# A fused LoRA matmul in five chunks of rows in place of six, with the weights loaded ahead of the first rows

## The chip, the cores and the metric

The kernel runs on one core of a Trainium2 chip. The metric is device time in microseconds (us), the median of several executions. One more execution is recorded by the hardware profiler; its span runs from the first to the last instruction, and its time on the device is a little longer than the span.

## The reference

`x` has 16 × 2048 = 32,768 rows of 256 fp32 numbers, `W` is 256 × 256, `lora_A` 256 × 16, `lora_B` 16 × 256, `lora_E` has 16 numbers, and `scale` is 1.0.

```python
x_flat = x.reshape(-1, in_dim)
y = x_flat @ W
lora_out = x_flat @ lora_A
lora_out = lora_out * lora_E
lora_out = lora_out @ lora_B
y = y + scale * lora_out
```

The output has the shape and type of `x`. So 33.55 MB are read, 33.55 MB are written, and the matmuls between them are small.

## The kernel before

**The mathematics.** The low-rank part is folded into the weights once: `weff = W + A diag(E·scale) B`, in bf16 (lines 148 to 167). After that the kernel is one matmul, `x @ weff`.

**Rows and chunks.** `PLAN` (line 5) cuts the 256 row groups into chunks. A row group is one row for each of the 128 partitions, 1 KB a partition, 131,072 bytes in all. A chunk of `b` row groups takes `b × 128` successive rows of `x`; partition p gets `b` neighbouring rows, so that a chunk is one run of `b` KB in each partition (line 51). In this text "48 rows" means 48 row groups, as in the plan. `PIECES` (line 7) cuts the load of a chunk into several DMAs: chunk 0 comes as 16 and 32 rows, chunk 2 as 24 and 24.

**Slots.** `SLOTS` (line 9) are the buffers in SBUF. A chunk is loaded into a slot, and its result is written over it there, so a slot is free again when its store has landed. `LEAD = 4` is the number of slots: chunks 0 to 3 are loaded at the start, chunk 4 goes into the slot of chunk 0, chunk 5 into that of chunk 1.

**The order of the DMAs** is written out by hand. All loads of x and all stores are issued by SP, and run in its queue one behind another. At the start come the first piece of chunk 0 (line 114), W (115), the second piece of chunk 0 (119) and chunks 1 to 3 (120, 121). The three small tensors go through ScalarE's queue (116 to 118). Later SP waits for each chunk's last result and issues its store (223, 224); `AFTER = {1: [4, 5]}` (line 11) says that right behind store 1 it waits until store 0 has landed, issues load 4, waits until store 1 has landed, and issues load 5 (225 to 227).

**Steps.** Compute goes in 32 steps of `S = 8` rows. In each step t:

- VectorE rounds 8 rows to bf16, `rounded(t)`, line 141. Where a loaded piece begins there, it waits for that piece's load (135).
- TensorE transposes them, seen as 32-bit words, into PSUM, `transposed`, line 180.
- VectorE copies the transposed words to SBUF, `copied(t)`, line 145.
- TensorE multiplies them by `weff`, 16 matmuls, `multiplied`, line 191.
- ScalarE copies the result out of PSUM into the slot, in two halves, line 214.

VectorE takes its work in the order written: round 0, the weights' sum, round 1, and then copy t, round t+2 for each t (164 to 172). TensorE transposes step t+1 ahead of multiplying step t (201 to 204), and the first multiplication waits for the sum of the weights (199).

**HOLD** (line 13, used at 136 to 140) makes VectorE stop ahead of rounding step 14 until store 1 has landed.

**The weights.** VectorE rounds `lora_B` (149), TensorE transposes `lora_A` (153), VectorE scales it by E (`ate`, 157), TensorE multiplies the two (162), and VectorE adds W (`weff`, 167), after a wait for W's load.

Of the kernel before, what the change touches and what calls it, by code (L numbers as in the profile page):

```python
# [3 lines left out]

PLAN = [48, 32, 48, 32, 48, 48]

PIECES = {0: [16, 32], 2: [24, 24]}

SLOTS = [48, 48, 48, 32]
LEAD = 4  # L10
AFTER = {1: [4, 5]}

HOLD = 14, 1

# [19 lines left out]
def kernel(tc, x, W, lora_A, lora_B, lora_E, scale, out):  # L34
# [6 lines left out]
    KC = K // P  # L41
    assert K == M and sum(PLAN) * P == N
    starts = [sum(PLAN[:i]) * P for i in range(len(PLAN))]

    steps = [(i, r) for i, b in enumerate(PLAN) for r in range(0, b, S)]
    NS = len(steps)
    assert NS % 2 == 0

    def rows_of(flat, i):
        b, r0 = PLAN[i], starts[i]  # L50
        return flat[r0:r0 + b * P, :].rearrange("(p b) k -> p b k", b=b)

    def sbuf(name, shape, dt):
        return nc.alloc_sbuf_tensor(name, shape, dt).ap()
# [3 lines left out]

    slots = [sbuf(f"xy{s}", [P, rows, K], FP32) for s, rows in enumerate(SLOTS)]
    a_sb = sbuf("a_sb", [P, KC, R], FP32)  # L60
# [21 lines left out]
    pieces = {}  # L82
    for i, b in enumerate(PLAN):
        parts = PIECES.get(i, [b])
        pieces[i] = [(sum(parts[:j]), n) for j, n in enumerate(parts)]
    s_ld = {(i, r): Count(nc, f"s_ld{i}_{r}") for i in pieces for r, n in pieces[i]}
    s_st = [Count(nc, f"s_st{i}") for i in range(len(PLAN))]
    s_id, s_set, s_v, s_t, s_m, s_y = (
# [7 lines left out]
    def slot(i):  # L96
        return slots[i % LEAD][:, :PLAN[i], :]

    def load(i, parts=None):
        for r, n in parts or pieces[i]:  # L100
            s_ld[i, r].by(nc.sync.dma_start(out=slot(i)[:, r:r + n, :], in_=rows_of(x_flat, i)[:, r:r + n, :]), 16)  # L101

    def store(i):
        s_st[i].by(nc.sync.dma_start(out=rows_of(out_flat, i), in_=slot(i)), 16)
# [6 lines left out]


    with tc.tile_critical(no_gpsimd_drain=True):  # L113
        load(0, pieces[0][:1])
        s_w.by(nc.sync.dma_start(out=w_sb, in_=W.rearrange("(p c) m -> p c m", c=KC)), 16)  # L115
        s_a.by(nc.scalar.dma_start(out=a_sb, in_=lora_A.rearrange("(p c) r -> p c r", c=KC)), 16)
        s_b.by(nc.scalar.dma_start(out=b_sb, in_=lora_B), 16)
        s_e.by(nc.scalar.dma_start(out=e_sb, in_=lora_E[:, None]), 16)
        load(0, pieces[0][1:])
        for i in range(1, LEAD):  # L120
            load(i)
    tc.close()
# [9 lines left out]
    def rounded(t):  # L132
        i, r = steps[t]
        if (i, r) in s_ld:
            nc.vector.wait_ge(s_ld[i, r].sem, 16)
        if t == HOLD[0]:

            for _ in range(10):
                nc.vector.engine_nop()
            nc.vector.wait_ge(s_st[HOLD[1]].sem, 16)  # L140
        nc.vector.tensor_copy(out=xb[t % 2], in_=slot(i)[:, r:r + S, :]).then_inc(can_t[t % 2], 1)  # L141
# [19 lines left out]
    for c in range(KC):  # L161
        aeb_done = nc.tensor.matmul(ps_aeb[:, c, :], ate[:, c, :], b_bf, start=True, stop=True)  # L162
    s_set.by(aeb_done)
    rounded(0)
    nc.vector.wait_ge(s_w.sem, 16)
    nc.vector.wait_ge(s_set.sem, 2)
    s_v.by(nc.vector.tensor_add(out=weff, in0=w_sb, in1=ps_aeb))  # L167
    rounded(1)
    for t in range(NS):
        copied(t)  # L170
# [39 lines left out]
    for i, r in [(i, r + g) for i, r in steps for g in range(0, S, G)]:  # L210
# [7 lines left out]
        else:  # L218
# [5 lines left out]
            store(i)  # L224
            for later in AFTER.get(i, []):
                nc.sync.wait_ge(s_st[later - LEAD].sem, 16)
                load(later)
# [46 lines left out]
```

## Time and profile before

| what | value |
|---|---|
| time, median of 3 runs | 162.2 us (162.17 to 162.8) |
| time of the profiled execution | 162.28 us |
| its span | 161.0 us |
| HBM read, written | 33.85 MB, 33.55 MB: 419 GB/s over the span |
| rounding 8 rows, VectorE, line 141 | 32 of 1217 ns |
| copy of transposed words, VectorE, line 145 | 32 of 1224 ns |
| copy of half a step's result, ScalarE, line 214 | 64 of 1015 ns |
| first issue of SP, last store issued, last store landed | 0.94, 133.3, 160.9 us |

The page of the profile gives for each engine the time in which it was busy and its share of the span. The line that begins with DMA cuts the span into 40 slices of 4.0 us; a digit is the mean busy share of the 16 DMA engines in tenths, and 9 is 90% or more. A DMA of this kernel is cut over the 16 engines, 8 partitions on each, one packet for each partition and one packet of 4 bytes that counts the engine's part as done. The DMA view also gives, for the issues in a stretch of time, the time from issue to landing, which is when the last engine's part counts. The chain that ended last is followed back from the last instruction to what released each step; it is read with care where a resource is busy without a pause.

### The profile page before, as it was taken

The page shows a single profiled execution, that of the slowest core. Times are in us where ns is not written, and L with a number is a line of the kernel's source. Part 1 is how long each engine was busy: PE and PEld are TensorE (multiplying, and loading weights), DVE is VectorE, ACT ScalarE, POOL GpSimd, SP SyncE. Part 2 cuts the span into 40 slices and gives each one's busy share as a digit, 9 for nine tenths or more (in the row PEclk, how much of TensorE's full clock was granted, in tenths as well). Part 3 has the DMA queues.
Part 4 walks back from the last instruction along what each step waited for, and adds up shares of the span by engine and source line. Part 5 has one row for each costly group of instructions (what it writes and reads, how often), then busy time and mean ns, then how long its engine had stood idle before and what let it go on. Part 6 is the DMA issues. An engine that isn't in the chain of part 4 may idle for free.

```text
span 161.0 us, 1875 instructions
## 1 busy us (share of the span) xinstructions
PE 93.4 (58%) x780; PEld 83.9 (52%) x780; DVE 76.6 (48%) x67; ACT 63.2 (39%) x65; POOL 0.7 (0%) x6
## 2 busy tenths in 40 slices
PE   0149389999999300000299999999999980000000
PEld 0037179999999200000279999999999970000000
DVE  0073198889895000000595989898989500000000
ACT  0300508686867400000026686767777681000000
POOL 0100000000000000000000000000000000000000
PEclk9999959999999965555559999999999999555555
DMA  5999999999999999999999999999999999999994
GB/s 146 403 470 472 399 423 440 403 446 434 452 407 391 454 476 415 391 440 407 476 452 415 440 403 476 440 393 427 440 411 423 407 485 415 440 452 452 391 440 208
DMA packets 2370, 67.42 MB, mean 419 GB/s; under 512 B 432, under 2 KB 448, under 8 KB 576
## 3 DMA queue, kind: packets, MB, share of 16 engines
q1 hardware_dynamic: 2160, 67.37, 97.9%
q10 hardware_dynamic: 208, 0.03, 0.1%
q14 instruction: 2, 0.02, 0.0%
HBM read 33.85 MB, written 33.55 MB: 419 GB/s over the span
## 4 chain that ended last, share of the span: by engine, by line
PE 47%; DMA 30%; ACT 2%; DVE 2%; SPq 1%; issue 0%
PE psum_y L191 31%; DMA out_dram<-xy 20%; PE psum_xt L180 17%; DMA xy<-in_x_dram 11%; ACT xy L214 2%; DVE xb L141 2%; SPq L115 0%; SPq L101 0%; SPq L123 0%; SPq L113 0%
## 5 line engine op out<-in xcount | busy, mean ns | idle before, releaser
L214 ACT COPY xy<-psum_y 128x1024 f32<-128x1024 f32 x64 | 61.9, 1015 | 64.0 <-PE psum_y L191 64.0
L191 PE MATMUL psum_y<-weff,xt 128*128 128x256 bf16 x512 | 64.6, 282 | 0.0
L191 PEld LDWEIGHTS psum_y<-weff,xt 128*128 128x128 bf16 x512 | 51.9, 101 | 7.2
L180 PE MATMUL psum_xt<-ident,xb 128*128 128x128 f32 x264 | 37.8, 291 | 29.8 <-DVE xb L141 29.8
L141 DVE CAST xb<-xy 128x2048 bf16<-128x2048 f32 x32 | 38.9, 1217 | 33.3 <-DMA out_dram<-xy 27.8
L180 PEld LDWEIGHTS psum_xt<-ident,xb 128*128 128x128 f32 x264 | 32.7, 151 | 31.4 <-DVE xb L141 31.1
L145 DVE COPY xt<-psum_xt 128x1024 f32<-128x1024 f32 x32 | 39.2, 1224 | 10.5 <-PE psum_xt L180 10.5
L153 PE MATMUL psum_xt<-ident,a_sb 128*16 128x128 f32 x2 | 0.6, 394 | 6.8 <-POOL ident L127 6.8
L149 DVE CAST b_bf<-b_sb 16x256 bf16<-16x256 f32 x1 | 0.3, 281 | 7.8 <-DMA b_sb<-in_lora_B_dram 7.8
L214 ACT ACT_TABLE_LOAD x1 | 1.3, 1283 | 6.1 <-PEq L123 6.1
L153 PEld LDWEIGHTS psum_xt<-ident,a_sb 128*16 128x16 f32 x2 | 0.1, 88 | 6.8 <-DMA a_sb<-in_lora_A_dram 6.8
L162 PE MATMUL psum_xt<-b_bf,ate 16*128 16x256 bf16 x2 | 0.6, 403 | 2.1 <-DVE ate L157 2.1
L162 PEld LDWEIGHTS psum_xt<-b_bf,ate 16*128 16x128 bf16 x2 | 0.1, 105 | 2.6 <-DVE ate L157 2.6
L157 DVE TENSOR_SCALAR ate<-psum_xt,e_sb 16x256 bf16<-16x256 f32 x1 | 0.5, 471 | 1.0 <-DMA e_sb<-in_lora_E_dram 1.0
L167 DVE TENSOR_TENSOR weff<-w_sb,psum_xt 128x512 bf16<-128x512 f32 x1 | 0.7, 668 | 0.0
L127 POOL TENSOR_SCALAR_AFFINE_SELECT ident<-ident 128x128 f32<-128x128 f32 x1 | 0.3, 293 | 0.2 <-POOL ident L125 0.2
L125 POOL MEMSET ident<- 128x128 f32 x1 | 0.2, 205 | 5.5 <-POOLq L123 5.5
L255 POOL MEMSET const-bfloat16-1.0<- 128x1 bf16 x1 | 0.1, 101 | 0.0
L255 POOL MEMSET const-uint8-127<- 128x1 uint8 x1 | 0.1, 101 | 0.0
L255 POOL MEMSET const-float32-0.0<- 128x1 f32 x1 | 0.1, 98 | 0.2 <-issue 0.2
L255 POOL MEMSET const-float32-1.0<- 128x1 f32 x1 | 0.1, 98 | 0.0
## 6 DMA issues: line engine op xcount, KB each, us to landing
out_dram<-xy SPq DMA_DIRECT2D x4, 6144.0 KB, 29.8
xy<-in_x_dram SPq DMA_DIRECT2D x3, 4096.0 KB, 26.8
xy<-in_x_dram SPq DMA_DIRECT2D x2, 6144.0 KB, 26.8
out_dram<-xy SPq DMA_DIRECT2D x2, 4096.0 KB, 30.7
xy<-in_x_dram SPq DMA_DIRECT2D x2, 3072.0 KB, 36.4
xy<-in_x_dram SPq DMA_DIRECT2D x1, 2048.0 KB, 8.2
w_sb<-in_W_dram SPq DMA_DIRECT2D x1, 256.0 KB, 8.3
a_sb<-in_lora_A_dram ACTq DMA_DIRECT2D x1, 16.0 KB, 5.5
```

The costliest lines, as they stand in the source:

```text
L127: s_id.by(nc.gpsimd.affine_select(out=ident, in_=ident, compare_op=mybir.AluOpType.not_equal, fill=1.0, base=0, pattern=[[-1, P]], channel ...
L141: nc.vector.tensor_copy(out=xb[t % 2], in_=slot(i)[:, r:r + S, :]).then_inc(can_t[t % 2], 1)
L145: nc.vector.tensor_copy(out=xt[t % 2], in_=ps_xt[t % 2]).then_inc(can_m, 1)
L149: s_v.by(nc.vector.tensor_copy(out=b_bf, in_=b_sb))
L153: at_done = nc.tensor.transpose(ps_at[:, c, :], a_sb[:, c, :], ident)
L157: s_v.by(nc.vector.tensor_scalar(out=ate, in0=ps_at, scalar1=e_sb, scalar2=float(scale), op0=mybir.AluOpType.mult, op1=mybir.AluOpType.mult))
L162: aeb_done = nc.tensor.matmul(ps_aeb[:, c, :], ate[:, c, :], b_bf, start=True, stop=True)
L167: s_v.by(nc.vector.tensor_add(out=weff, in0=w_sb, in1=ps_aeb))
L180: done = nc.tensor.transpose(ps_xt[k][:, j, :], words[k][:, j, :], ident)
L191: done = nc.tensor.matmul(ps_y[h][:, j, :], pairs[k][:, h * G + j, :, c], weff[:, c, :], start=(c == 0), stop=(c == KC - 1))
L214: y = nc.scalar.copy(out=slot(i)[:, r:r + G, :], in_=ps_y[h])
L255: nc = _bacc.Bacc("TRN2", target_bir_lowering=False, num_devices=1)
```

## The change

The plan has five chunks. The first is loaded as 24 and 32 rows, each other one in one piece; chunk 2 had two. There are three slots of 56, 48 and 56 rows (160 in all) in place of four (176). The first three chunks, 160 rows as before, are loaded at the start; chunk 3 goes into the slot of chunk 0, chunk 4 into that of chunk 1, behind store 1 as before. W is issued ahead of all of x. In VectorE's order the sum of the weights comes ahead of rounding 0 in place of behind it. Steps stay 32, and HOLD stays at step 14 and store 1; chunk 2 now begins at step 13, chunk 3 at step 20, chunk 4 at step 26.

```diff
-PLAN = [48, 32, 48, 32, 48, 48]
+PLAN = [56, 48, 56, 48, 48]
 
-PIECES = {0: [16, 32], 2: [24, 24]}
+PIECES = {0: [24, 32]}
 
-SLOTS = [48, 48, 48, 32]
-LEAD = 4
-AFTER = {1: [4, 5]}
+SLOTS = [56, 48, 56]
+LEAD = 3
+AFTER = {1: [3, 4]}
...
     with tc.tile_critical(no_gpsimd_drain=True):
-        load(0, pieces[0][:1])
         s_w.by(nc.sync.dma_start(out=w_sb, in_=W.rearrange("(p c) m -> p c m", c=KC)), 16)
...
-        load(0, pieces[0][1:])
+        load(0)
         for i in range(1, LEAD):
             load(i)
...
     s_set.by(aeb_done)
-    rounded(0)
     nc.vector.wait_ge(s_w.sem, 16)
     nc.vector.wait_ge(s_set.sem, 2)
     s_v.by(nc.vector.tensor_add(out=weff, in0=w_sb, in1=ps_aeb))
+    rounded(0)
     rounded(1)
```

## The prediction

> **What bounds the kernel now.** I read the busy shares first, then the DMA part, then the chain that ended last, then the SP queue's own times.
>
> ```profile
> PE 93.4 (58%) x780; PEld 83.9 (52%) x780; DVE 76.6 (48%) x67; ACT 63.2 (39%) x65; POOL 0.7 (0%) x6
> ...
> DMA  5999999999999999999999999999999999999994
> ...
> q1 hardware_dynamic: 2160, 67.37, 97.9%
> ```
>
> No engine is busy above 58%, but SP's DMA queue (q1) fills the 16 DMA engines for 97.9% of the 161.0 us span, and no slice between the first and the last is below 9. The kernel moves its bytes without a hole. So only three things can change the time: how long the same bytes take, when the first packet moves, and a hole.
>
> The chain names matmuls for 47%, which misleads. This is its middle (start, duration, what):
>
> ```profile
> 45.00 1.94 ACT xy L214 x2
> 46.94 0.02 issue
> 46.95 31.40 DMA out_dram<-xy
> 78.35 0.02 issue
> 78.38 1.24 DVE xb L141
> 79.61 0.04 issue
> 79.66 1.97 PE psum_xt L180 x8
> 81.63 3.41 PE psum_y L191 x16
> 85.04 0.89 PE psum_xt L180 x8
> 85.93 1.75 PE psum_y L191 x16
> ```
>
> Store 1 is issued at 46.95 and lands at 78.35, because it stands behind two loads and a store. HOLD lets rounding 14 start only then. After it the first step runs at half clock (1.97 + 3.41 us) and later ones at full clock (0.87 + 1.75 = 2.62 us a step). Compute ends at 133.3 and the queue works to 161.0: PE's share of the chain is time beside DMA work.
>
> The issues of the SP queue (start, stretch they fall in, count) show how early each is:
>
> ```profile
> 36.47 10.82 SPq L104 DMA_DIRECT2D out_dram<-xy  x2
> 68.63 10.07 SPq L101 DMA_DIRECT2D xy<-in_x_dram  x2
> 91.42 42.25 SPq L104 DMA_DIRECT2D out_dram<-xy  x4
> ```
>
> One issue at a time, the DMA view gives the time to landing. Issue plus that time is the landing: the first 16 rows 9.1, W 9.7, the next 32 rows 19.4, chunk 1 at 29.1, chunk 2 at 43.7, chunk 3 at 54.2; store 0 at 68.6, store 1 at 78.35; load 4 at 92.8, load 5 at 107.8; stores 2 to 5 at 122.2, 131.9, 146.4 and 160.9. The differences price a DMA behind another: 48 rows 14.50 (load 4, stores 2, 4, 5: 14.45 to 14.52), 32 rows 9.68. That is 0.3013 us a row and 0.04 us a DMA. Two differences stand out, both of the last load before a store: chunk 3 took 10.5 in place of 9.68 (0.8 more), load 5 took 14.94 (0.4 more).
>
> **The change, part by part.**
>
> *Fewer, larger DMAs.* Rows are the same 512 (256 in, 256 out); W is the same. Loads of x fall from 8 to 6, stores from 6 to 5: three DMAs fewer at 0.04, so 0.12 us by the fit. The packets say a little more: a row group of a partition is one packet, 1213 ns for 32 KB and 1815 ns for 48 KB, so some 9 ns a packet besides the bytes. With 8 packets on each engine and a closing semaphore packet of 9 ns, a DMA costs 0.08 us: 0.24 for three. I take 0.24, because it is worked from the packets themselves and the small loads (24 rows: 7.3 us, where the fit gives 7.27) lean that way. A 56-row packet (56 KB) isn't in the trace. By extension it is 2.12 us, 16.9 us a DMA; 16 KB (611 ns) to 48 KB lie on one line, so I take it.
>
> The Trainium skill, "DMA: Bandwidth & Descriptors", section "Anatomy of one DMA", gives each DMA about 2.0 us fixed besides its bytes; by that, three DMAs would be 6 us. The rows show 0.04 to 0.08 behind another DMA, so I leave the 6 us to a rival.
>
> *W ahead of x.* The first packet moves at 2.2 us, 1.27 after its issue; the two first DMAs are issued 0.43 apart (0.94, 1.37) and W's share is 0.70 on an engine. W's packets (84 ns) will meet the slow start that x meets now (first packets of 0.6 to 2.0 us in place of 0.61). x's descriptors follow 0.43 later, W covers 0.70, so I take nothing. If x's packets are late despite W, it costs up to the 0.43; if W hides in the start-up, it saves up to 0.70 − 0.43 = 0.27.
>
> *Weights' sum ahead of the first rounding.* VectorE waits in order, so rounding 0 and all behind it now stand behind W, and behind e through `ate` and the two small matmuls. W lands earlier. e lands at 9.0 now, its packets taking turns with x's packets of 0.61 us; beside 24 KB packets (0.91) the time after the first packet grows at most in that ratio: 2.2 + 6.8 × 0.91/0.61 = 12.3. From e's landing to the end of the sum it is about 1.9 (0.47 `ate`, 0.60 matmuls, 0.67 sum, hand-overs), so 14.2 at worst, while 24 rows land at 9.7 + 8 × 0.3013 = 12.1. Rounding 0 may be 2 us late; three steps at 2.62 still end their part before the next rows land at 21.8. The cost is nothing: the store that these steps feed has over 10 us to spare (next part).
>
> *New plan.* I lay the landings again, keeping the measured extras. x's 24 rows 12.1, then 32 rows 21.8, chunk 1 (48) 36.3, chunk 2 (56, last load before a store, +0.8) 54.0. Store 0 70.8, store 1 85.4, load 3 99.9, load 4 (+0.4) 114.8, store 2 131.7, store 3 146.2, store 4 160.7. That is 0.24 below 160.9, with no hole. For each store I check that it is issued in time. From issue to first packet it is 1.3, and the fastest engine is ahead of the landing by 1.4 early and 1.8 late (the packets that close a DMA lie that far apart).
>
> - Store 0: the rounding that waits for the second piece moves from 19.4 to 21.8, and one step more hangs on the first piece; the four steps behind are as before, so 36.47 + 2.4 = 38.9. Needed at 51: 12 to spare.
> - Store 1: step 13's rounding now waits for chunk 2 at 54.0; behind it in VectorE's queue stands step 12's copy out of PSUM, and for that wait TensorE, ScalarE and the store. From a rounding after a pause to the ScalarE copies of the step before it the timeline shows 7.7 (78.38 to 86.09, half clock): 61.7. Needed at 68: 6 to spare. Loads 3 and 4 keep their place behind store 1; load 3 is issued at 70.8 with store 1 still running to 85.
> - HOLD is still step 14 and store 1: 85.4 in place of 78.35, with the same compute queued behind. Store 2 then is step 19, four steps later than step 15 was: 85.4 + 13.04 (78.38 to 91.42 now) + 4 × 2.62 = 108.9. Needed at 114.8 − 1.8 − 1.3 = 111.7: **2.8 to spare, where it had 13**. Rounding 20 comes at 85.4 + 16.6 = 102.0 (94.97 now, 16.6 behind rounding 14) and load 3 lands at 99.9; rounding 26 at 117.7, load 4 at 114.8.
> - Store 3 at 124.6 (needed at 128.6), store 4 at 140.3 (needed at 143.1): 2.8 again for the last.
>
> *The change from loads to stores.* At 50 to 54 us the chip loses its 0.8, and compute is still running there:
>
> ```profile
> 50.00:54.00 4.00, 3.70 (x34) 3.15 (x32) 0.59 (x1) 3.07 (x4) 0.00 (x0) 1.00 0.97 369
> 54.00:58.00 4.00, 0.00 (x0) 0.00 (x0) 0.00 (x0) 0.79 (x1) 0.00 (x0) 0.96 1.00 432
> ```
>
> (Columns: PE, PEld, DVE, ACT, POOL busy, clock, DMA share, GB/s: 369 against 432.) In the new plan VectorE waits there for chunk 2 and compute mostly stands. If compute makes the loss, up to 0.8 goes; if the loss goes with the packet (56 KB for 32 KB), it grows to 1.4, 0.6 more. The trace doesn't tell. The change at 78, without a loss, is from stores to loads, and the one at 106 costs 0.4 with compute running and larger packets, nearest to "unchanged". I take 0.
>
> **The sum** is made against the profiled execution, 162.28 us (span 161.0 and 1.28 around it), which is 0.08 above the median of 162.2: 162.28 − 0.24 = **162.0 us**. That is 0.1% below the median: no change, since about 0.5% (0.8 us, so 161.4 to 163.0) is what a measurement of this kernel can tell.
>
> **Rivals.**
>
> 1. *The change to stores gets cheap.* With compute idle at 50 to 54 us the 0.8 goes: 161.2, and 161.0 with W hidden in the start. For it: the change without compute (78 us) lost nothing. Against: that one goes the other way. Chance 0.13.
> 2. *Slower: store 2 late for the queue.* It decides when store 2 is issued after 111.7. A clock window at half speed that stays costs: a step is 1.97 + 3.41 = 5.38 against 2.62, so 3.4 us of half clock lose 1.75. The pause after store 1 ends in 5.5 us of half clock now (79.7 to about 85.2); with two windows more the slip is 3.5, the hole 0.7; with three, 5.25 and 2.45, 164.5 us. Against: the clock was full from the first busy window on. The Trainium skill, "TensorE: Matmul & The Clock Gate", section "Part 1: The HAM clock gate", has the clock full after one busy window of some 3.4 us at an unsteady phase; by that rule, the rows agree, no third window would come. A load 3 that lands over 2.1 us late would do the same through rounding 20, which holds step 19's copy. Chance 0.17, the larger as the spare times of stores 2 and 4 and of load 3 all fall to between 2 and 3.
> 3. *A fixed cost for each DMA that the queue doesn't hide.* 6 us less: 156.3. Against: 0.04 between neighbours, and 32 and 48 rows on one line. Chance 0.02.
> 4. *W ahead does nothing:* e, not W, sets the weights' sum. This is inside my forecast.
>
> My forecast has 0.68. Faster: rivals 1 and 3, 0.15; slower 0.18 (rival 2, and 0.01 for start and packets at their upper ends together); same 0.67. **The range** takes in the unknown costs: 162.0 − 0.8 = 161.2 below; 162.0 + 0.43 + 0.6 = 163.0, rounded up to 163.1, above.
>
> **What would show it.** Landing differences of 16.9 for 56 rows, 14.5 for 48; the queue never below 9 tenths; store 2 issued near 108.9 and load 4 landed near 114.8; GB/s at 50 to 54 near 370 (rival 1: near 430). A DMA slice of 7 or 8 near 113 us, and store 2 issued past 111.7, would be rival 2 and prove me wrong; so would 24 rows that land past 12.5.

## The result and the profile after

The changed kernel takes 162.65 us in the median (162.34 to 163.08), the kernel before 162.3 on the same chips (162.14 to 162.8). The ratio is 1.002, with an interval from 1.0013 to 1.0027. It is slower by 0.35 us: little, inside the range, but clear of chance and against the 0.24 us saved that I forecast. So 0.6 us are to be found.

The profiled execution of the changed kernel took 163.08 us (span 161.7), 0.43 above its median; one more, in the experiments, took 162.48 (span 161.2). Lines of the page of the changed kernel that answer to those of before:

```profile
PE 94.2 (58%) x780; PEld 83.5 (52%) x780; DVE 76.5 (47%) x67; ACT 63.2 (39%) x65; POOL 0.8 (1%) x6
...
DMA  4999999899997999999999999999999999999991
GB/s 170 468 464 397 389 571 401 389 421 454 454 454 227 454 456 454 454 389 413 498 425 401 401 474 450 425 401 446 399 454 454 440 391 474 450 425 401 438 474 73
...
q1 hardware_dynamic: 1728, 67.37, 97.1%
```

The packets are fewer (1728 for 2160), and by their own records no engine pauses for more than 0.1 us between two of them from 12 us on, so the queue never runs empty. The slice that stands out is the 13th, 48.5 to 52.5 us, with 227 GB/s; the stretch that the forecast named, where it expected some 370 GB/s, reads 244:

```profile
50.00:54.00 4.00, 4.00 (x39) 3.71 (x38) 1.66 (x3) 2.77 (x3) 0.00 (x0) 1.00 0.58 244
```

That view gives a packet's bytes to the stretch in which it begins, so its figures jump by a packet for each engine; the closer look below is by the packets' own records. No hole opened behind that stretch: stores were issued where the forecast had them. The issues (start, stretch, count), then the last three stores one at a time (size, time to landing):

```profile
42.96 16.87 SPq L104 DMA_DIRECT2D out_dram<-xy  x2
70.95 14.82 SPq L101 DMA_DIRECT2D xy<-in_x_dram  x2
109.32 31.77 SPq L104 DMA_DIRECT2D out_dram<-xy  x3
```

```profile
out_dram<-xy SPq DMA_DIRECT2D x1, 7168.0 KB, 22.9
...
out_dram<-xy SPq DMA_DIRECT2D x1, 6144.0 KB, 22.2
...
out_dram<-xy SPq DMA_DIRECT2D x1, 6144.0 KB, 20.9
```

Store 2 is issued at 109.32 (forecast 108.9), store 3 at 125.04 (124.6), store 4 at 140.76 (140.3). With the other issues taken the same way, the landings beside the forecast are:

| landing of | forecast | profiled |
|---|---|---|
| first 24 rows | 12.1 | 11.8 |
| 32 rows | 21.8 | 21.4 |
| chunk 1 | 36.3 | 35.9 |
| chunk 2 | 54.0 | 53.9 |
| store 0, store 1 | 70.8, 85.4 | 71.0, 85.4 |
| load 3, load 4 | 99.9, 114.8 | 100.3, 114.7 |
| store 2 | 131.7 | 132.2 |
| store 3 | 146.2 | 147.2 |
| store 4 | 160.7 | 161.7 |

Two things are to be seen. The loads begin 0.3 to 0.4 ahead of the forecast and have lost that by the end of chunk 2. And the last engine's part loses about 1 us in stores 2 and 3, where the forecast had full speed.

**The first: a slow stretch ahead of the first store.** The trace has a record of every packet, and each DMA closes with one 4-byte packet on each of the 16 engines. The mean over the engines of these closing packets tells how long a load took without the accident of the slowest engine. "Loss" below is this mean duration of the last load ahead of store 0, less what its rows cost elsewhere (32 rows 9.68, 56 rows 16.91). Before, it is 0.58 us; in the changed kernel 1.03, and 0.92 in its second profile.

**The second: one slow engine.** An engine's packets can be followed, since each begins where the last one ended. Of the changed kernel's 56 KB packets of store 2, all but a few take 2116 ns; one engine, and only one, takes this long (start us, KB, ns):

```
114.17 56 2141     123.00  56 2225     131.94 48 1914
116.31 56 2225     125.22  56 2244     133.85 48 1914
118.53 56 2234     127.46  56 2225     135.76 48 1928
120.76 56 2239     129.68  56 2258     137.68 48 1952
```

It is 5 to 7% slow until about 140 us, where compute ends (ScalarE's last copy ends at 140.7), and collects 1.3 us. The kernel before has the same: an engine with 1905 to 1924 ns for 1815 from 107.9 on, until compute ends at 133.3, 1.4 us in all. But that engine happened to be 0.5 ahead of the mean when the last stores began, and ended 0.1 ahead of the last engine. In the changed kernel's two profiles it was 0.43 behind and 0.27 ahead of the mean, and ended 1.69 and 1.08 behind it.

Over all 16 engines the mean end is 159.87 before and 159.76 and 159.80 after. The last engine ends at 160.82 before, and 161.46 and 161.00 after.

### The profile page after: what moved, and what is told of

Read it like the earlier page. It is cut to its first block, busy times and chain, and to the rows that moved or that the text cites. A ratio compares the mean times of both kernels' runs of the same rounds, so it can differ in the third digit from the quotient of the medians.

```text
span 161.7 us, 1868 instructions
## 1 busy us (share of the span) xinstructions
PE 94.2 (58%) x780; PEld 83.5 (52%) x780; DVE 76.5 (47%) x67; ACT 63.2 (39%) x65; POOL 0.8 (1%) x6
## 3 DMA queue, kind: packets, MB, share of 16 engines
q1 hardware_dynamic: 1728, 67.37, 97.1%
## 4 chain that ended last, share of the span: by engine, by line
PE 33%; DMA 16%; ACT 2%; DVE 1%; issue 0%
PE psum_y L190 22%; DMA out_dram<-xy 16%; PE psum_xt L179 11%; ACT xy L213 2%; DVE xb L140 1%
## 5 line engine op out<-in xcount | busy, mean ns | idle before, releaser
L140 DVE CAST xb<-xy 128x2048 bf16<-128x2048 f32 x32 | 38.9, 1219 | 41.2 <-DMA out_dram<-xy 29.1
```

## The experiments

Each ratio is to the kernel before on the same chip, in brackets its interval. Chips differ (the kernel before had medians from 162.3 to 162.82 on them), so only ratios are compared; single times stand beside a run of the kernel before. The loss is of one profile each.

**Which part of the change costs?** The plan alone, which is the changed kernel with the old start (the lines are against the changed kernel):

```diff
     with tc.tile_critical(no_gpsimd_drain=True):
+        load(0, pieces[0][:1])
         s_w.by(nc.sync.dma_start(out=w_sb, ...), 16)
...
-        load(0)
+        load(0, pieces[0][1:])
...
+    rounded(0)
     nc.vector.wait_ge(s_w.sem, 16)
...
-    rounded(0)
     rounded(1)
```

> The new plan with the old start: x's first piece ahead of W, rounding 0 ahead of the weights' sum. Theory A (the change from loads to stores at 50 to 54 us costs more than before, about 1.0 us in the mean of the engines in place of 0.6, because the last load before it is one packet of 56 KB on each partition in place of 32 KB; the start gains some 0.3): 162.9, slower than the changed kernel by 0.3, GB/s at 50 to 54 us near 325. Theory B (the plan saves its 0.24 and W ahead of x costs): 162.0, faster than the changed kernel by 0.6. Theory C (neither part; one DMA engine that falls behind sets the end, by chance of the layout): within 0.1 of the changed kernel, 162.6.

Measured: ratio 1.0011 (1.0001 to 1.002), loss 0.95.

And the start alone, the same lines the other way on the kernel before:

> The old plan of six chunks with the new start: W ahead of x, the weights' sum ahead of rounding 0. Theory A: the first 16 rows and W land 0.3 earlier and nothing else changes: 162.0. Theory B: 162.9. Theory C: 162.3.

Measured: ratio 1.0012 (1.0002 to 1.0023), loss 0.77. The first 16 rows and W were in at 8.71 in the mean, for 8.88 before. So each part costs about 0.1%, and together they make the 0.2%. In time, theory C comes nearest for the plan alone and none fits the start; A's gain and B's gain are in neither. What is slower in both is the last engine and not the mean: the mean end is 159.88 and 159.73, for 159.87 before, and the last engine ends at 161.16 and 161.00, for 160.82.

**Is it the last load's packet?** The changed kernel with chunk 2 in two loads, 24 and 32 rows, and 48 and 8:

```diff
-PIECES = {0: [24, 32]}
+PIECES = {0: [24, 32], 2: [24, 32]}
```

> The changed kernel with chunk 2 loaded as 24 and 32 rows, so that the last load before the first store has packets of 32 KB as in the kernel before. Theory A: the loss at 50 to 54 us falls from 1.0 to 0.6, one DMA more costs 0.08: 162.3, no slower than the kernel before. Theory B and theory C: 162.7, as the changed kernel.

> The changed kernel with chunk 2 loaded as 48 and 8 rows: the last load before the first store has packets of 8 KB. Theory A, if the loss goes with the packet: 0.15 in place of 1.0, less 0.08 for a DMA more, 161.9. If the loss is a fixed stretch of time ahead of the first store: 162.6 to 162.7, and the packets of 48 KB before the last are slow too. Theories B and C: 162.7.

Measured: ratios 1.0019 (1.0011 to 1.0028) and 1.0023 (1.0014 to 1.0032), losses 1.08 and 0.82. Theory A falls: the loss doesn't go with the packet. The 8 KB packets show its shape (rate of all engines by their records, in GB/s, over the quarter of a microsecond that begins at the time given):

```
us     49.75 50.25 50.75 51.25 51.75 52.25 52.75 53.25
GB/s     428   422   342   285   218   242   375   433
```

For two microseconds ahead of the first store's first packet, at about 52.8, the loads run at down to half speed, and the store then runs at full speed.

**Does the slow engine set the end?** Both kernels without compute in the last two chunks:

```diff
-    steps = [(i, r) for i, b in enumerate(PLAN) for r in range(0, b, S)]
+    steps = [(i, r) for i, b in enumerate(PLAN) for r in range(0, b, S) if i < 3]
...
                 load(later)
+    for i in range(3, len(PLAN)):
+        spent(nc.sync, s_ld[i, 0])
+        store(i)
...
```

> The changed kernel without the compute of chunks 3 and 4 (steps 20 to 31 are left out; stores 3 and 4 write x back), so that no engine works beside the last stores. All DMAs stay. Theory D (one of the 16 DMA engines is 5 to 6% slow while stores run beside compute, collects 1.3 us there, and ends last): that engine ends with the others, 162.65 - 0.5 to - 0.9 = 161.8 to 162.1, and no packet of 56 or 48 KB after 114 us is slow. Rival (the loss is the slow stretch ahead of the first store alone): 162.6, since that stretch stays.

The other has `i < 4` in the same places:

> The same for the kernel before: chunks 4 and 5 (steps 20 to 31) without compute. Theory D: in its profile the slow engine ended only 0.1 ahead of another engine that is late for other reasons, so 162.2 to 162.1; the two kernels without this compute then stand closer than 0.35 apart, with the changed one at most 0.1 slower. Rival (slow stretch): 162.3, and the difference of 0.35 stays.

Measured: ratios 0.9982 (0.9955 to 1.0009) and 0.9986 (0.9965 to 1.0006). In the profile without compute, the 56 KB packets of store 2 all take 2116 ns and the 48 KB packets 1815: the slow engine is gone, which shows that work of the engines beside the stores makes it slow. What that costs in time is less clear. The two kernels now stand level (0.9982 against 0.9986), as theory D has it, but on this chip the intervals are wide enough to hide the 0.2% that was between them, and neither ratio is clear of 1. The changed kernel's ratio with compute is 1.002, so leaving the compute out does make it faster, if ratios carry from chip to chip. The slow engine is not all of the lag either: without it the last engine still ends 1.09 us behind the mean in the changed kernel and 1.45 in the kernel before. The ends of the engines are 1.6 and 2.1 us apart, now from the loads ahead of store 2, where some engines lost over 1 us at the second change from loads to stores.

**A time, or the change itself?** 176 rows ahead of the first store, and a small store early in the changed kernel:

```diff
-PLAN = [48, 32, 48, 32, 48, 48]
+PLAN = [48, 48, 48, 32, 48, 32]
```

> The kernel before with the plan 48, 48, 48, 32, 48, 32: 176 rows are loaded ahead of the first store in place of 160, so that the change from loads to stores falls near 57.5 us. If the slow stretch belongs to the change: GB/s near 430 at 50 to 53 us and near 350 at 55 to 58. If it belongs to a time after the start: near 370 at 50 to 54 as before and 430 at 55 to 58. Time near 162.3 either way.

```diff
         load(0)
+        nc.sync.wait_ge(s_w.sem, 16)
+        s_dm.by(nc.sync.dma_start(out=rows_of(out_flat, 4)[:, 0:KC, :], in_=w_sb), 16)
         for i in range(1, LEAD):
             load(i)
...
```

> The changed kernel with a store of W's 256 KB (into rows that store 4 overwrites later) behind the second load, near 20.7 us. If the slow stretch is paid once, by the first store of the execution: it is seen at 18 to 21 us, and the one at 50 to 54 us is gone (430 GB/s). If it is paid at each change from loads to a waiting store: at both places. If it hangs on the place after 160 rows: at 50 to 54 us alone. Time 162.65 + 0.65 for the added bytes, and up to 1.0 more in the second case.

Measured, the kernel before taking 162.64 on that chip: with 176 rows 162.45 us, full speed (429 to 433) up to 56 us and 361 to 402 from 56 to 58; the loss is 0.30. With the early store 163.43 us: a loss of 0.24 ahead of it, at 18 to 21 us, and 0.42 at the old place. So the stretch belongs to a change from loads to a waiting store, wherever it is. It isn't paid once, though the two changes together cost less than the one did.

**The spread of the engines, the first store's packet, chance.**

```diff
         load(0)
+        s_sp.by(nc.sync.dma_start(out=scratch, in_=rows_of(x_flat, 4)[:8, 0:SP_ROWS, :]), 16)
         for i in range(1, LEAD):
...
```

> The changed kernel with a small load of 8 partitions x 20 KB into a scratch buffer behind the second load, which only 8 of the 16 DMA engines carry: those fall 0.75 us behind the others. Theory E (the loss at the change from loads to the first store is large when the engines reach it together, 0.5 to 0.9 us apart as in the changed kernel, and small when they are spread by about 1 us as in the kernel before): the engines reach it 1.2 to 1.6 us apart, and the mean loss falls from 1.0 to 0.3 or less. Theory F (the loss goes with the first store's packets, 56 KB against 48 KB) or none: 0.9 to 1.1.

```diff
-        s_st[i].by(nc.sync.dma_start(out=rows_of(out_flat, i), in_=slot(i)), 16)
+        for r, n in ([(0, 24), (24, 32)] if i == 0 else [(0, PLAN[i])]):
+            s_st[i].by(nc.sync.dma_start(out=rows_of(out_flat, i)[:, r:r + n, :], in_=slot(i)[:, r:r + n, :]), 16)
...
```

> The changed kernel with store 0 in two DMAs of 24 and 32 rows: the first store's packets are 24 KB in place of 56. Theory F: the mean loss at the change falls from 1.0 to below 0.5. Theory E: it stays near 1.0, as the engines are as close together as before.

```diff
-PLAN = [48, 32, 48, 32, 48, 48]
+PLAN = [56, 24, 48, 32, 56, 40]
-PIECES = {0: [16, 32], 2: [24, 24]}
+PIECES = {0: [24, 32], 2: [24, 24]}
-SLOTS = [48, 48, 48, 32]
+SLOTS = [56, 40, 48, 32]
```

> The kernel before with chunks of 56, 24, 48, 32, 56, 40 rows: x ahead of W, six chunks, four slots and a last load of 32 rows as before, but the first store has packets of 56 KB. Theory F: the mean loss at the change is near 1.0. Theory E: 0.2 to 0.6 as in the kernel before, with the engines about 0.95 apart.

> The changed kernel once more, for a second profile. If the loss belongs to the kernel: a mean loss of 0.9 to 1.2 at the change from loads to stores, and the slow engine 1.3 us behind by the end. If it is chance of one execution: anywhere from 0.2 to 1.3.

Measured, with a run of the kernel before at 162.71: spread 164.73 us, and a loss of 0.03; store 0 in two 162.91, loss 1.09; first56 162.08, loss 0.20; the changed kernel again 162.48, loss 0.92. The small load cost far more than its bytes, 2.5 us in the mean before the last load began (eight packets to eight neighbouring partitions), so that run moves the whole change later and not only the engines apart; they were 0.96 apart at its start. Theory F falls twice, by store 0 in two and by first56. Theory E falls by first56, whose engines were 0.63 apart, closer than in the changed kernel. The loss belongs to the kernel: 1.03 and 0.92.

**When store 0 is issued, and whether store 1 waits behind it.** The kernel before with one of the two held back, and the changed kernel with store 0 earlier:

```diff
             nc.sync.wait_ge(s_y.sem, done)
+            if i == 0:
+                nc.sync.wait_ge(s_ld[2, 24].sem, 16)
             store(i)
```

> The kernel before, with store 0 held back in SP until the second half of chunk 2 has landed (43.6 us), so that it is issued 9.5 us ahead of the end of the loads in place of 16; store 1 follows at 47 as before. Theory H (the slow stretch at the change is long where store 0 is issued late, some 10 us ahead): mean loss 0.9 or more in place of 0.2 to 0.6. Theory G (it is long where store 1 does not stand in the queue yet): 0.2 to 0.6.

The second waits at store 1 in the same way, for chunk 3:

> The kernel before, with store 1 held back in SP until chunk 3 has landed (54 us), so that only store 0 stands in the queue at the change, as in the changed kernel. Theory G: mean loss 0.9 or more. Theory H: 0.2 to 0.6.

```diff
-PIECES = {0: [24, 32]}
+PIECES = {0: [24, 32], 1: [24, 24]}
```

> The changed kernel with chunk 1 loaded as 24 and 24 rows, so that the rounding that begins chunk 1 does not wait until 35.8 us and store 0 is issued near 36 us in place of 43, 17 us ahead of the end of the loads. Theory H: mean loss 0.2 to 0.6 in place of 1.0, time 162.65 - 0.5 + 0.08 = 162.2. Theory G: 1.0, and 162.7.

Measured, the kernel before taking 162.62 on that chip: store 0 issued at 43.87, loss 0.52, 162.44 us; store 1 issued at 54.57, loss 0.61, 162.85; store 0 issued at 37.37 in the changed kernel, loss 1.03, ratio 1.0004 (0.9991 to 1.0017). Theories H and G both fall. The last of these tells one thing more. Its stretch from 50 to 53 us, and the changed kernel's (columns as in the forecast):

```profile
50.00:53.00 3.00, 0.00 (x0) 0.00 (x0) 0.00 (x0) 0.44 (x1) 0.00 (x0) 1.00 0.61 249
```

```profile
50.00:53.00 3.00, 3.00 (x30) 2.81 (x29) 1.62 (x2) 2.31 (x3) 0.00 (x0) 1.00 0.56 229
```

TensorE and VectorE stand still in the one and work in the other, and the loss is 1.03 in both: compute doesn't make it.

**The chunk that the last load comes from, the candidate, and its start.**

```diff
-PLAN = [48, 32, 48, 32, 48, 48]
+PLAN = [48, 32, 24, 56, 48, 48]
-PIECES = {0: [16, 32], 2: [24, 24]}
+PIECES = {0: [16, 32]}
-SLOTS = [48, 48, 48, 32]
+SLOTS = [48, 48, 24, 56]
```

> The kernel before with chunks of 48, 32, 24, 56, 48, 48 rows: six chunks, four slots, x ahead of W, store 0 of 48 rows, all as before, but the last load ahead of the first store is a chunk of 56 rows in one piece, so that its 128 packets lie 56 KB apart in HBM. Theory J (the slow stretch at the change is long where the last load comes from a chunk of 56 rows, whatever its packets): mean loss 0.8 to 1.2 as in the changed kernel, and 0.3 to 0.5 slower than the kernel before. Theory K (it hangs on something else of the five-chunk plan, such as its three slots): 0.2 to 0.6, and within 0.15 of the kernel before.

> Once more the plan 56, 24, 48, 32, 56, 40 with the old start, timed and for a second profile: it lost 0.16 at the change and ran 162.08 in its one look. If that belongs to the plan: again 0.1 to 0.3 lost, a span below 160.9 and a median near 162.0. If it was chance: 0.2 to 0.8 and 162.3, as the kernel before.

With the new start, the lines of the change besides:

> The plan 56, 24, 48, 32, 56, 40 with the new start (W ahead of x, the weights' sum ahead of rounding 0). If the new start costs by itself, as the two medians of the old plan say: a ratio to the kernel before of 0.9975 to 0.998 in place of the 0.9964 of the same plan with the old start. If that cost was chance: 0.996 or less, for the first loads land 0.1 to 0.3 earlier.

Measured: last56 ratio 1.0 (0.9984 to 1.0017), loss 0.56; first56 timed 0.9964 (0.9952 to 0.9977), loss 0.55 (its first profile's loss, 0.16 in the expectation, is 0.20 by the measure of this text); the same with the new start 0.9975 (0.9963 to 0.9987), loss 0.95. Theory J falls. The new start costs 0.1% on this plan as on the old one. And the plan 56, 24, 48, 32, 56, 40 with the old start beats both kernels, by 0.4% the one before and so, by the two ratios, by some 0.6% the changed one. Its two profiles have their loads in at 52.76 and 52.95, against 53.14 before, and a mean end of 159.36 and 159.55, against 159.87. Why it loses less was not found out. These two profiles also show how far executions of one kernel differ: they took 162.08 and 162.90 us, with the last engine 1.10 and 1.90 behind the mean.

**What all profiles say together.** The mean time at which the 160 rows ahead of store 0 would have been in without the loss, and the loss:

| kernel | would end | loss | | kernel | would end | loss |
|---|---|---|---|---|---|---|
| tail_after | 52.04 | 1.26 | | first56_timed | 52.40 | 0.55 |
| store_two | 52.09 | 1.09 | | before | 52.56 | 0.58 |
| after | 52.14 | 1.03 | | first56 | 52.56 | 0.20 |
| third_two | 52.14 | 1.08 | | late_s0 | 52.62 | 0.52 |
| early_s0 | 52.15 | 1.03 | | late_s1 | 52.63 | 0.61 |
| after_again | 52.18 | 0.92 | | last56 | 52.63 | 0.56 |
| last_small | 52.21 | 0.82 | | tail_before | 52.67 | 0.23 |
| first56_start | 52.27 | 0.95 | | spread (with 8 × 20 KB more) | 54.63 | 0.03 |
| plan_only | 52.29 | 0.95 | | | | |
| start_only | 52.35 | 0.77 | | | | |

By and large, the earlier the loads would end, the longer the stretch: but for spread, all are in between 52.76 and 53.30, whatever was saved ahead of that point. The two clean pairs agree: the new start brought the loads forward by 0.21 in start_only against before, and by 0.13 in first56_start against first56_timed, and the loss grew by 0.19 and 0.40 (against first56's other profile by 0.29 and 0.75). This is a regularity over 17 profiles, not a cause. No run moved the start alone by a set amount, and what holds the end near 53.1 stays open.

## Why the prediction was wrong

**What bounds the kernel** was right: the queue is full before and after, and stores 2 to 4 were issued 0.4 to 0.5 us after the times that I gave, within their spare 2.8. Rival 2 did not happen.

**Fewer, larger DMAs.** Right in mechanism: stores of 56 rows take 16.91 on the fastest engine (forecast 16.9), of 48 rows 14.50. The size of the saving is nearer to the 0.12 of my fit than to the 0.24 that I took: with 9.68 for 32 rows, these intervals still give 0.04 us a DMA, and the balance below leaves 0.10 to 0.13 for this term. Rival 3 is out, since one DMA behind another costs under a tenth of a microsecond. The Trainium skill, "DMA: Bandwidth & Descriptors", section "Anatomy of one DMA", with its fixed 2.0 us a DMA, would have had the kernel 6 us faster; that section describes DMAs that GpSimd issues, and puts most of the 2.0 us down to the wait for confirmation that the last byte has landed. All DMAs of x here are issued by SP, and no run here shows such a cost added for each DMA of a full queue.

**W ahead of x.** "I take nothing" was wrong in size: W hid in the start-up, and the first rows came 0.3 us earlier than laid out (0.2 to 0.3 in the mean of the engines), near the 0.27 that I had as the most it could save. Its price was not in my account at all: the new start alone makes the kernel 0.12% slower (1.0002 to 1.0023).

**Weights' sum.** Right that it costs nothing. It starts at 9.35 and the first rounding at 11.76 waits for x:

```profile
8.10 0.47 DVE L156 TENSOR_SCALAR ate<-psum_xt,e_sb 16x256 bf16<-16x256 f32 x1 [3.10 <-DMA e_sb<-in_lora_E_dram]
...
9.35 0.69 DVE L165 TENSOR_TENSOR weff<-w_sb,psum_xt 128x512 bf16<-128x512 f32 x1 [0.77 <-PE psum_xt L161]
11.76 2.37 DVE L140 CAST xb<-xy 128x2048 bf16<-128x2048 f32 x2 [1.73 <-DMA xy<-in_x_dram]
```

**The new plan's times.** Store 0 was issued at 42.96, not 38.9: I had missed that rounding 7 begins chunk 1 and waits for it to 36.0, with step 6's copy queued behind it. That was covered, as 12 us were to spare.

```profile
36.01 1.23 DVE L140 CAST xb<-xy 128x2048 bf16<-128x2048 f32 x1 [5.36 <-DMA xy<-in_x_dram]
```

"Compute mostly stands" at 50 to 54 us was wrong too: the row of 50 to 54 us shows TensorE busy for 4.00 of 4.00 us. It made no difference to the loss (early_s0).

**The change from loads to stores** is the step of the sum that failed, as I put it: "I take 0." Its loss grew from 0.58 to 0.92 and 1.03 us in the two profiles, and so gave back some 0.4 of what the start and the DMAs had saved. That chunk 2 landed at 53.9 us for the forecast 54.0 was luck: a start 0.3 too late in my sum and a loss 0.4 too small cancelled. I had the growth as an upper end of 0.6, but tied to the packet's size, and third_two, last_small, store_two and first56 take that away. Rival 1 (compute makes the loss) falls as well.

**What no step held.** I priced the queue by one landing after another, as if the 16 engines were one. The end is that of the last engine, and one engine is slow wherever the last stores run beside compute: it collects 1.3 to 1.5 us there in the profiles with 160 rows ahead of store 0 and with that compute, and 1.8 in t176. How far this shows hangs on where that engine stood before. In the two profiles of the changed kernel it, or an engine hit elsewhere, ended 1.69 and 1.19 behind the mean, for 0.94 before.

So the account of the 0.6 us is this, in the mean of the 16 engines and then for the last one (the two profiles of the changed kernel against the one of the kernel before, gains positive):

| term | us |
|---|---|
| new start, at the first rows | 0.30, 0.20 |
| change from loads to stores | −0.45, −0.34 |
| second change, ahead of store 2 (a loss of 0.16 before; 0, 0.08) | 0.16, 0.08 |
| what is left for the three DMAs fewer | 0.10, 0.13 |
| mean end of the engines | 0.11, 0.07 |
| last engine behind the mean | −0.75, −0.25 |

Of the 0.59 us by which I missed, the means thus hold only 0.13 to 0.17 (0.07 to 0.11 gained in place of 0.24), because the loss at the change was in part made up by the start. The rest, some 0.4, must be in the last engine. That is an estimate from the medians and these profiles: the lag of the last engine differs between executions of one kernel by half a microsecond and more, in three kernels that are close to the kernel before it was 1.06, 1.41 and 0.92 us (late_s0, late_s1, last56), and its share is not settled. Nor is its cause: the slow engine is part of it, and both kernels lag without it too. early_s0 has the changed kernel's loss of 1.03, a last engine only 1.00 behind and a ratio of 1.0004, which fits this account.

Last, "about 0.5% is what a measurement of this kernel can tell" was too wide: 22 runs of each kernel gave the ratio to within 0.07%.

## What to carry to other kernels

Where one DMA queue is full from end to end, a saving ahead of some point may be taken back at the next change of direction, as most of it was in the changed kernel; compare the mean end of all engines at each such point, not only the first and last landing. Price the end by the last of the 16 engines. Compute beside the last stores slows one of them; whether it pays to keep it from there was not shown. Below half a per cent, take each part of a change alone: here two parts that each bring the loads forward each made the kernel slower.

## What the runs showed of the hardware

- A load followed in its queue by a waiting store is slowed ahead of the store's first packet, to half speed for about 2 us (218 GB/s at 51.75 in last_small); at a store followed by a load most engines lose nothing (14.50 for 48 rows). The second change of an execution costs less: 0.16 in the kernel before, 0 and 0.08 in the changed one, 0.27 and 0.31 in the two kernels without compute at the end.
- In 17 profiles with 160 rows ahead of the first store, the loss is by and large the larger the earlier the loads would have ended, 0.2 to 1.3 us.
- One of the 16 DMA engines takes 1914 for 1815 ns and 2234 for 2116 ns in stores beside compute, and no more than the others without it. The Trainium skill, "DMA: Bandwidth & Descriptors", section "Latency and other measured facts", has two of the engines as usually slower and guesses at descriptor rings of DMAs issued by GpSimd. No DMA of this kernel is issued by GpSimd, only one engine is slow, and only beside compute, so the runs agree that engines differ but not with that guess; the trace gives engines no numbers.
- A load of 8 partitions × 20 KB, 160 KB in all, delayed the following load's end by 2.5 us in the mean of 16 engines (37.72 in place of 20.66 + 14.53), where its bytes alone would cost 0.4.
